# A tuned two-block network on one core: 276 matrix products of zeros in thirteen forms, emitted behind the last store

## The chip, the cores and the metric

The kernel runs on one core of a Trainium2 chip. The time is device microseconds of one execution. Five engines work side by side in a core, each in the order of its own queue: PE (TensorE) multiplies matrices, and its weight loads are listed apart as PEld; DVE (VectorE) and ACT (ScalarE) do elementwise work; POOL (GpSimd) and SP (SyncE) mostly issue transfers. Engines wait for each other on semaphores.

## The reference

Two networks run one after the other on 256 tokens of width 1024, all in float32. The first has two layers of feed-forward, neighbourhood attention with a pooling path, and feed-forward again. The second has four layers, each a mixer (gated linear attention, latent attention, convolution, gated linear attention), an MLP and a gated per-layer input. Its end, cut to what the change touches:

```python
# last layer of the second network, i = 3
x = layer_norm(ALPHA * x + mlp(x))                       # relu(x w1)^2 w2
x = x + sigmoid(x @ ple_w_gate_2[i]) * (p_2[i] @ ple_w_proj_2[i])
return x                                                 # [1, 256, 1024], float32
```

The reference holds no further product: what the change adds is no part of the result.

## The kernel before

The 256 tokens are two tiles of 128 partitions. Every large product is done three times on PE to keep float32 accuracy: each operand is split into a high and a low part of type float32r (ACT copies the high part at L169 or L174, DVE subtracts at L170 or L175), and `mm3` (L177 to L182) adds high times high (L180), high times low (L181) and low times high (L182) into one PSUM bank. A product here is one instruction: `lhsT`, the stationary operand, is loaded as weights, `rhs`, the moving operand, is streamed through. `gemm_rows` holds 128 tokens as weights and streams up to 512 columns of a weight matrix; `gemm_cols` holds 128 columns of a weight matrix and streams 256 or 512 tokens. Other products are of plain float32: the transposes, the attention scores, and the sums at L356.

The order on each engine comes from a scheduler that lets ready work of a lower place in the program go between work of a higher one. SBUF and PSUM come from pools, and a pool opened later gets the space of one that was closed, so its first write waits for the last reader there.

The program is `net.block1()` and then `net.block2()`. The last thing of block 2 is `ple` (L911 to L930) for layer 3, in two halves of 512 columns, each over both token tiles. At its end, for the last 512 columns of the second tile:

```python
nc.scalar.activation(sg[:, gs], ps[t][:, gs], AF.Sigmoid)                # L922, ACT
nc.vector.tensor_mul(sg[:, gs], sg[:, gs], pe[t][:, os])                 # L923, DVE
nc.vector.tensor_add(self.rows[t][:, os], self.rows[t][:, os], sg[:, gs])  # L924, DVE
nc.sync.dma_start(self.out[0, t * P:(t + 1) * P, os], self.rows[t][:, os])  # L926, SP
```

They run on pieces of 256 columns, so twice for each token tile. After the last store the engines meet in a closing exchange of semaphores, listed under the line of the program's end (L1303 before, L1341 after).

Of the kernel before, what the change touches and what calls it, by code (L numbers as in the profile page):

```python
# [18 lines left out]
P = 128  # L19
# [17 lines left out]
def _constants():  # L37
    """Arrays that depend on shapes alone."""
    c = {}
# [59 lines left out]
class Net:  # L99
# [28 lines left out]

# [1 line left out]
    def tick(self, n=1):  # L130
# [7 lines left out]
    def fbank(self):  # L138
        """Either kind of bank in turn."""
        self.turn = not self.turn  # L140
        return self.bank() if self.turn else self.xbank()
# [19 lines left out]
    def halves(self, v, shape=None, tag=""):  # L161
        """The exact split of v into two float32r parts."""
        kn, cn = v.shape[1], v.shape[2]
        out = []
        for nm in ("hi", "lo"):
            t = self.w.tile([P, 1024], F32R, tag="w" + nm + tag, name="w" + nm, bufs=self.SPL)
            out.append(t[:, :kn * cn].rearrange("p (k c) -> p k c", k=kn))
        hi, lo = out
        self.nc.scalar.copy(hi, v)  # L169
        self.nc.vector.tensor_sub(lo, v, hi.bitcast(F32))  # L170
        return hi, lo
# [5 lines left out]
    def mm3(self, ps, a, b, first, last):  # L177
        """ps += a^T b with both as (hi, lo) pairs."""
        mm = self.nc.tensor.matmul
        mm(ps, lhsT=a[0], rhs=b[0], start=first, stop=False)  # L180
        mm(ps, lhsT=a[0], rhs=b[1], start=False, stop=False)  # L181
        mm(ps, lhsT=a[1], rhs=b[0], start=False, stop=last)  # L182

    def gemm_cols(self, ps, w, x, c0, cn):
        """ps[feature, token] over all k: w hi/lo [P, k, 128], x hi/lo [P, k, tokens]."""
        kn = w[0].shape[1]
        for k in range(kn):
            self.mm3(ps, (w[0][:, k, :], w[1][:, k, :]),
                     (x[0][:, k, c0:c0 + cn], x[1][:, k, c0:c0 + cn]), k == 0, k == kn - 1)

    def gemm_rows(self, w, kn, c0, cn, x, tiles, per=4, major=2, order=None, bank=None):
        """Banks [token, column] for each tile; w is a DRAM matrix with kn k-tiles.

        The last major loads are taken tile by tile, so that the first tiles end early."""
        ps = [(bank or self.bank)() for _ in tiles]
# [22 lines left out]
    def rstd_of(self, ms, eps):  # L218
        """(ms + eps)^-1/2; eps may be a column."""
        nc = self.nc  # L220
        v = self.small.tile([P, 1], F32, tag="v", name="v")
        if isinstance(eps, float):
            nc.gpsimd.tensor_scalar(v, ms, eps, None, ALU.add)
        else:
            nc.gpsimd.tensor_tensor(v, ms, eps, ALU.add)
        r = self.small.tile([P, 1], F32, tag="r", name="r", bufs=8)
        nc.gpsimd.tensor_tensor(r, v, self.neg_half, ALU.pow)
        return r

    def rstd_of_two(self, ms):  # L230
        """The same from the two halves' mean squares."""
        m0 = self.small.tile([P, 1], F32, tag="m0", name="m0")
        self.nc.gpsimd.tensor_scalar(m0, ms[0], EPS, None, ALU.add)
        return self.rstd_of(ms[1], m0)

    def meansq(self, src, n):
        """The sum of squares over n, a power of four."""
        ms = self.small.tile([P, 1], F32, tag="ms", name="ms", bufs=8)
        j = self.tmp.tile([P, 1024], BF16, tag="junk", name="junk", bufs=1)
        self.nc.scalar.activation(j[:, :src.shape[-1]], src, AF.Square, scale=float(n ** -0.5), accum_out=ms)  # L240
        return ms

    def columns(self, rows, n, pool, name):
        """[n, 128] rows -> [128, n]."""
        ps = self.tbank()
# [5 lines left out]
    def to_columns(self, rows, hi, lo, c0, nblk):  # L251
        """rows: list of tiles [P, nblk*128]; hi/lo [P, block, token] at c0 get the transposes."""
        nc = self.nc
# [10 lines left out]

# [1 line left out]
    def block1(self):  # L266
# [42 lines left out]
    def mod_raw(self, l, v, k0):  # L309
        """Rows of k-tiles k0, k0+1 for vector v."""  # L310
        return self.load(self.d["w_mod"][l, k0 * P:(k0 + 2) * P, v * D:(v + 1) * D]
                         .rearrange("(k p) c -> p k c", p=P), 2, D)

    def mod_pair(self, l, v):
        """Vectors v and v+1 by matrix products; bank rows 32j (x) and 32j+1 (ctx) for half j."""
        nc = self.nc
# [14 lines left out]
    def mod_units(self, l, vectors):  # L331
        """Steps that form the vectors by sums on the vector engine over k, then over partitions."""
        nc = self.nc
# [35 lines left out]
    def mod_finish(self, l, acc, rows):  # L369
        """From the bank rows (row, vector, half, stream): + b_mod, (1 + scale) g, gate g."""  # L370
        nc, d = self.nc, self.d
# [43 lines left out]
    def modulated(self, l, i, groups):  # L415
        """hT hi/lo [P, 8, tokens] of the modulated norm i for groups of token tiles, each after its tail."""
        nc = self.nc
# [37 lines left out]
    def sooner(self, on=True):  # L455
        """Puts a chain that others wait for ahead of the products around it."""
        return self.tc.high_priority(offset=SOONER) if on else ExitStack()

    def later(self, by):
        """Lets products fill what the chains emitted after them leave free."""  # L460
        return self.tc.high_priority(offset=-by)

    def add_normed(self, t, y, ms):
        """x += y * rstd, y already times the gate row."""
        nc = self.nc
# [78 lines left out]
    def gate_up_rows(self, l, w, hT, hid):  # L544
        """Blocks 0 and 1 token by token, so that tile 0 goes ahead."""
        nc = self.nc
# [16 lines left out]
    def gate_up(self, l, w, f0, fn):  # L563
        """The split gate and up columns of blocks f0..f0+fn, in turn."""
        wgu = self.d["w_ffn_gate_up"][l, w]
# [96 lines left out]
    def stacks(self, hp, mp, q, k):  # L662
        """Heads 2hp and 2hp+1 on partitions: q as (hi, lo), (lo, hi) and k as hi twice; k's lo parts in place."""
        nc = self.nc
# [25 lines left out]
    def attend(self, l, s, hp, mp, stacks, vu, cat):  # L690
        """Heads 2hp and 2hp+1 of stream s: local and context keys for x, context keys for ctx."""
        nc = self.nc
# [29 lines left out]
    def softmax_T(self, sc, nk, scale, mp, dst):  # L722
        """Softmax over the free axis of sc, transposed in blocks into dst [P, nk, 128]."""
        nc = self.nc
# [18 lines left out]
    def na_bias(self, l, hp, t, mp):  # L743
        """[P queries, head, 256 keys]: rpb laid out over the window, -1e30 outside it."""
        nc = self.nc
# [35 lines left out]

# [1 line left out]
    def block2(self, layers=(0, 1, 2, 3)):  # L783
# [39 lines left out]
    def rows_to_xT(self, t, b0, b1, x):  # L823
        """Blocks b0..b1 of token tile t into x."""
        for b in range(b0, b1, 4):
# [15 lines left out]
    def layer_norm(self, i, j, gemm):  # L841
        """x = norm(ALPHA x + gemm); returns x transposed, hi/lo."""
        nc, d = self.nc, self.d
# [28 lines left out]
    def mlp_hidden(self, i, hp, x):  # L872
        """relu(x w1)^2 transposed, hi/lo; the first columns token by token, so that tile 0 goes ahead."""
        nc, d = self.nc, self.d
# [21 lines left out]
    def ple_in(self, i):  # L896
        """The transposed per-layer input, hi/lo."""
        nc, d = self.nc, self.d
# [12 lines left out]
    def ple(self, i, pe, x, last):  # L911
        """x += sigmoid(x w) * pe; returns the new x transposed, or stores it."""
        nc, d = self.nc, self.d
# [17 lines left out]
    def gla(self, j, mp, x):  # L931
# [60 lines left out]
        def scores(h):  # L992
            """Decayed scores of head h [key, query] within each tile and across the two."""
            self.ph = ph + "_rec"
# [101 lines left out]
    def rotate(self, dst, src, cs, t, nh, mp):  # L1096
        """dst, src [P, nh*64]."""
        nc = self.nc
# [13 lines left out]
    def mla(self, j, mp, x):  # L1112
# [23 lines left out]
        def rope_key():  # L1136
            """The rotated key part of all heads, twice over the partitions."""
            ps = self.tbank()
# [22 lines left out]
        def up(raws, off, width):  # L1161
            """hi/lo [P, 8 heads, width] of the head columns at off, for both k-tiles."""
            return [self.halves(raw[:, 0, :].rearrange("p (h c) -> p h c", h=8)[:, :, off:off + width])
# [40 lines left out]
        def scores(h):  # L1204
            """The softmax of head h, keys on partitions."""
            self.ph = ph + "_att"
# [40 lines left out]
    def conv(self, j, mp, x):  # L1247
# [27 lines left out]
        return cat  # L1275


_NAMES = [
# [20 lines left out]
def _program(nc, arrays):  # L1299
# [3 lines left out]
    with tile.TileContext(nc) as tc, ExitStack() as ctx:  # L1303
        net = Net(ctx, tc, d, out)
        net.block1()
        net.block2()


# [9 lines left out]
```

## Time and profile before

| what | value |
|---|---|
| time, median of 2 runs | 3036.41 us (3034.1 to 3038.72) |
| profiled execution: span from first to last instruction | 3045.1 us |
| PE busy | 2980.0 us, 98% of the span |
| DVE, ACT, POOL busy | 1875.6, 1281.8, 288.6 us |
| mean granted TensorE clock | 0.994 of full speed |
| end of the last product of the program | 3040.4 us into the span |

Of the profiled execution only the span is given, not a time of its own; it is one more execution beside the two timed ones. The span lies 8.7 us (0.3%) over the median of those. Full speed of the clock is 2.4 GHz, and its other level is 1.2 GHz, shown as 0.5.

### The profile page before, as it was taken

How to read it: one execution, taken by the hardware profiler on the slowest of the kernel's cores; microseconds unless marked ns; L12 is line 12 of the kernel's file. 1: busy time of each engine (PE TensorE's matmuls, PEld its weight loads, DVE VectorE, ACT ScalarE, POOL GpSimd, SP SyncE). 2: the span in 40 equal slices, each digit the busy share in tenths (PEclk: the TensorE clock that was granted, in tenths of full speed). 3: DMA queues.
4: the chain of work that ended last, by engine and by line, in shares of the span. 5: the costliest groups of instructions: out<-in, count | busy, mean ns of one | idle time of the engine just before them, and what ended most of it. 6: DMA issues, size and time to landing. Idle time of an engine off the chain costs nothing.

```text
span 3045.1 us, 40666 instructions
## 1 busy us (share of the span) xinstructions
PE 2980.0 (98%) x16362; PEld 2481.3 (81%) x16362; DVE 1875.6 (62%) x2454; ACT 1281.8 (42%) x1876; POOL 288.6 (9%) x480
## 2 busy tenths in 40 slices
PE   7999999999999999999999999999999999999999
PEld 5777777787778877787789888987798989887997
DVE  5757765577553775336655567656664776467755
ACT  3222245442222422224654465546453545355543
POOL 2101030011110110001100121000000000002000
PEclk9999999999999999999999999999999999999999
DMA  7555531245543454333345536554455565553654
GB/s 280 179 175 180 187 107 63 91 155 180 170 132 110 149 181 154 99 98 120 97 160 186 176 130 192 187 181 165 131 184 187 183 201 183 186 194 111 198 180 145
DMA packets 321936, 484.70 MB, mean 159 GB/s; under 512 B 16606, under 2 KB 199442, under 8 KB 320340
## 3 DMA queue, kind: packets, MB, share of 16 engines
q1 hardware_dynamic: 307844, 461.75, 46.2%
q0 software_dynamic: 9296, 16.16, 1.6%
q10 hardware_dynamic: 4608, 4.20, 0.5%
q8 instruction: 128, 2.10, 0.3%
q14 instruction: 60, 0.49, 0.0%
HBM read 480.97 MB, written 1.10 MB: 158 GB/s over the span
## 4 chain that ended last, share of the span: by engine, by line
PE 89%; DVE 5%; POOL 2%; ACT 2%; DMA 1%; issue 1%; SPq 0%; ACTq 0%; DVEq 0%; POOLq 0%
PE ffn_gu L180 9%; PE ffn_gu L182 9%; PE ffn_gu L181 9%; PE mlp L181 7%; PE mlp L180 7%; PE mlp L182 7%; PE ffn_dn L182 4%; PE ffn_dn L181 4%; PE ffn_dn L180 4%; PE m L180 3%; PE m L182 3%; PE m L181 3%; DVE wlo L170 2%; PE mix_in L181 1%; PE mix_in L180 1%; PE mix_in L182 1%
## 5 line engine op out<-in xcount | busy, mean ns | idle before, releaser
L170 DVE TENSOR_TENSOR wlo<-raw,whi 128x1024 fp32r<-128x1024 f32 (+1 forms) x735 | 884.9, 1211 | 636.6 <-ACT whi L169 621.6
L169 ACT CAST whi<-raw 128x1024 fp32r<-128x1024 f32 (+1 forms) x735 | 760.7, 1038 | 1129.9 <-PE ffn_gu L181 290.7
L181 PE MATMUL ffn_gu<-hT_lo,whi 128*128 128x512 f32 (+1 forms) x1472 | 524.5, 357 | 1.8 <-DVE hT_lo L175 1.8
L180 PE MATMUL ffn_gu<-hT_hi,whi 128*128 128x512 f32 (+1 forms) x1472 | 525.7, 358 | 0.5 <-ACT hT_hi L174 0.5
L182 PE MATMUL ffn_gu<-hT_hi,wlo 128*128 128x512 f32 (+1 forms) x1472 | 523.8, 356 | 0.7 <-DVE wlo L170 0.7
L180 PEld LDWEIGHTS ffn_gu<-hT_hi,whi 128*128 128x128 f32 x1472 | 277.7, 189 | 52.9 <-ACT whi L169 4.2
L181 PEld LDWEIGHTS ffn_gu<-hT_lo,whi 128*128 128x128 f32 x1472 | 278.1, 189 | 43.8 <-DVE hT_lo L175 2.4
L182 PEld LDWEIGHTS ffn_gu<-hT_hi,wlo 128*128 128x128 f32 x1472 | 277.8, 189 | 43.7 <-DVE wlo L170 1.3
L347 DVE SCALAR_TENSOR_TENSOR macc<-raw,sil,macc 128x1024 f32<-128x1024 f32 x224 | 274.6, 1277 | 42.9 <-DMA raw<-in_w_mod_dram 42.9
L180 PE MATMUL mlp<-xT_hi,whi 128*128 128x256 f32 x896 | 253.9, 283 | 0.0
L181 PE MATMUL mlp<-xT_lo,whi 128*128 128x256 f32 x896 | 253.8, 283 | 0.0
L182 PE MATMUL mlp<-xT_hi,wlo 128*128 128x256 f32 x896 | 253.5, 283 | 0.0
L180 PE MATMUL ffn_dn<-whi,hid_hi 128*128 128x512 f32 x616 | 244.1, 396 | 0.0
L181 PE MATMUL ffn_dn<-wlo,hid_hi 128*128 128x512 f32 x616 | 243.6, 395 | 0.0
L182 PE MATMUL ffn_dn<-whi,hid_lo 128*128 128x512 f32 x616 | 243.5, 395 | 0.0
L180 PE MATMUL mlp<-whi,mlp_hi 128*128 128x512 f32 x512 | 199.2, 389 | 0.0
L181 PE MATMUL mlp<-wlo,mlp_hi 128*128 128x512 f32 x512 | 199.2, 389 | 0.0
L182 PE MATMUL mlp<-whi,mlp_lo 128*128 128x512 f32 x512 | 199.2, 389 | 0.0
L181 PEld LDWEIGHTS mlp<-xT_lo,whi 128*128 128x128 f32 x896 | 172.0, 192 | 0.0
L182 PEld LDWEIGHTS mlp<-xT_hi,wlo 128*128 128x128 f32 x896 | 172.0, 192 | 0.0
L180 PEld LDWEIGHTS mlp<-xT_hi,whi 128*128 128x128 f32 x896 | 172.0, 192 | 0.0
L180 PEld LDWEIGHTS ffn_dn<-whi,hid_hi 128*128 128x128 f32 x616 | 115.9, 188 | 29.3 <-ACT yrow L489 2.5
(402 smaller groups left out, 4794.5 us busy)
## 6 DMA issues: line engine op xcount, KB each, us to landing
raw<-in_mlp_w_dram SPq DMA_DIRECT2D x128, 1024.0 KB, 5.4
raw<-in_w_ffn_gate_up_dram SPq DMA_DIRECT2D x80, 1024.0 KB, 5.3
raw<-in_w_mod_dram SPq DMA_DIRECT2D x72, 1024.0 KB, 5.2
raw<-in_w_ffn_down_dram SPq DMA_DIRECT2D x32, 1024.0 KB, 5.1
raw<-in_gla_w_in_dram SPq DMA_DIRECT2D x24, 1024.0 KB, 5.2
raw<-in_w_in_dram SPq DMA_DIRECT2D x16, 1024.0 KB, 5.0
raw<-in_ple_w_gate_dram SPq DMA_DIRECT2D x16, 1024.0 KB, 5.2
raw<-in_w_ffn_down_dram SPq DMA_DIRECT2D x16, 768.0 KB, 4.6
```

The costliest lines, as they stand in the source:

```text
L169: self.nc.scalar.copy(hi, v)
L170: self.nc.vector.tensor_sub(lo, v, hi.bitcast(F32))
L180: mm(ps, lhsT=a[0], rhs=b[0], start=first, stop=False)
L181: mm(ps, lhsT=a[0], rhs=b[1], start=False, stop=False)
L182: mm(ps, lhsT=a[1], rhs=b[0], start=False, stop=last)
L347: nc.vector.scalar_tensor_tensor(acc[s], raw[:, k - k0, :], c, acc[s], ALU.mult, ALU.add)
```

## The change

A method `probe` is added, and called once after `net.block2()`. It takes four float32r tiles and two bf16 tiles of 1056 columns, sets all to zero on DVE, and issues thirteen groups of products on them into PSUM banks that nobody reads. The groups differ in the starting column of the operands (0 or 8), their type, the number of streamed columns (512 or 256), of weight columns (128 or 64), of contracted partitions (128, 64, or 64 alternating between the lower and the upper half), the number of banks, and whether one pair of operands is used throughout or several in turn. Elsewhere the diff replaces comments and docstrings by empty lines, which moves nothing.

```diff
+    def probe(self):
+
+        nc = self.nc
+        self.ph = "probe"
+        with ExitStack() as ctx:
+            pool = lambda name, bufs, **k: ctx.enter_context(self.tc.tile_pool(name=name, bufs=bufs, **k))
+            pp = pool("probe", 1)
+            ps = pool("probe_ps", 6, space=PSUM)
+            a, b, c, e = (pp.tile([P, 1056], F32R, name="pr" + n) for n in "abce")
+            u, v = (pp.tile([P, 1056], BF16, name="pr" + n) for n in "uv")
+            for t in (a, b, c, e, u, v):
+                nc.vector.memset(t.bitcast(F32) if t.dtype == F32R else t, 0.0)
+            bank = lambda: ps.tile([P, 512], F32, tag="probe", name="probe")
+
+            def run(name, n, lhs, rhs, out=None, banks=1):
+                bs = [bank() for _ in range(banks)]
+                for i in range(n):
+                    o = bs[i % banks]
+                    o = o if out is None else out(o)
+                    nc.tensor.matmul(o, lhsT=lhs(i), rhs=rhs(i), start=i < banks, stop=i >= n - banks)
+
+            run("p0", 20, lambda i: a[:, 0:128], lambda i: c[:, 0:512])
+            run("p1", 20, lambda i: a[:, 0:128], lambda i: c[:, 8:520])
+            run("p2", 20, lambda i: a[:, 8:136], lambda i: c[:, 8:520])
+            run("p3", 20, lambda i: a[:, 8:136], lambda i: c[:, 0:512])
+            run("p4", 20, lambda i: u[:, 0:128], lambda i: v[:, 0:512])
+            run("p5", 24, lambda i: a[:, 8:136], lambda i: c[:, 8:264], out=lambda o: o[:, :256])
+            run("p6", 20, lambda i: a[:, 8:72], lambda i: c[:, 8:520], out=lambda o: o[:64, :])
+            run("p7", 20, lambda i: a[:, 0:128], lambda i: c[:, 0:512], banks=2)
+            run("p8", 20, lambda i: a[:64, 0:128], lambda i: c[:64, 0:512])
+            run("p9", 20, lambda i: a[64 * (i % 2):64 * (i % 2) + 64, 0:128],
+                lambda i: c[64 * (i % 2):64 * (i % 2) + 64, 0:512], banks=2)
+            run("p10", 24, lambda i: u[:, 0:128], lambda i: v[:, 0:256], out=lambda o: o[:, :256])
+            run("p11", 24, lambda i: (a, b)[i % 2][:, 128 * (i % 8):128 * (i % 8) + 128],
+                lambda i: (c, e)[i % 2][:, 512 * (i // 2 % 2):512 * (i // 2 % 2) + 512])
+            run("p12", 24, lambda i: (a, b)[i % 2][:, 8 + 128 * (i % 8):8 + 128 * (i % 8) + 128],
+                lambda i: (c, e)[i % 2][:, 8 + 512 * (i // 2 % 2):8 + 512 * (i // 2 % 2) + 512])
...
         net.block1()
         net.block2()
+        net.probe()
```

On DVE, at the very end of the program, the difference is this; `sgm` is the sigmoid's tile, `xr` the rows that are stored, `pra` to `prv` the six new tiles:

```order
 L923 TENSOR_TENSOR sgm<-sgm,pe 128x256 [waits Activation_49] x2
 L924 TENSOR_TENSOR xr<-xr,sgm 128x256 [waits DVE_49] x2
+L1288 MEMSET pra 128x1056 [waits PE_49]
 L923 TENSOR_TENSOR sgm<-sgm,pe 128x256 [waits Activation_49] x2
 L924 TENSOR_TENSOR xr<-xr,sgm 128x256 [waits DVE_49] x2
-L1303 UNCONDITIONAL_BRANCH
+L1288 MEMSET prb 128x1056
+L1288 MEMSET prc 128x1056
+L1288 MEMSET pre 128x1056
+L1288 MEMSET pru 128x528
+L1288 MEMSET prv 128x528
```

The first memset has come ahead of the last four elementwise operations of the program, and the other five follow them.

On PE, at the same place, with the waits; `ple` is the bank of the last products of the program, `probe` a new bank, `pru` and `prv` the bf16 tiles:

```order
 L182 MATMUL ple_25273<-whi,xT_lo 128x512
-L1303 UNCONDITIONAL_BRANCH
+L1296 MATMUL probe<-prc,pra 128x512 [waits DVE_49,PE_49,Activation_49]
+L1296 MATMUL probe<-prc,pra 128x512 x79
+L1296 LDWEIGHTS pru [waits DVE_49]
+L1296 MATMUL probe<-prv,pru 128x512 [waits DVE_49]
+L1296 LDWEIGHTS pru
```

All new products stand behind the last product of the program, group after group; the first one waits for DVE and ACT, and the bf16 ones have a weight load that stands as an instruction of its own.

## Rows read from the trace of the kernel before

**Rows 1.** The page's head and its section 1, busy us by engine:
```profile
span 3045.1 us, 40666 instructions
PE 2980.0 (98%) x16362; PEld 2481.3 (81%) x16362; DVE 1875.6 (62%) x2454; ACT 1281.8 (42%) x1876; POOL 288.6 (9%) x480
```

**Rows 2.** Timeline from 3036 us: start us, us, engine line operation [idle before]:
```profile
3036.16 0.39 PE L180 MATMUL ple<-whi,xT_hi 128*128 128x512 f32 x1
...
3040.01 0.39 PE L182 MATMUL ple<-whi,xT_lo 128*128 128x512 f32 x1
3040.44 0.66 ACT L922 ACTIVATE sgm<-ple 128x256 f32<-128x256 f32 x2 [4.78 <-PE ple L182]
3040.86 0.76 DVE L923 TENSOR_TENSOR sgm<-sgm,pe 128x256 f32<-128x256 f32 x2 [4.01 <-ACT sgm L922]
3041.53 0.76 DVE L924 TENSOR_TENSOR xr<-xr,sgm 128x256 f32<-128x256 f32 x2
```

**Rows 3.** The stores' line: duration ns min/median/max, first and last start us:
```profile
L926 SPq DMA_DIRECT2D out_dram<-xr x8: 332/372/433, 3026.1 to 3042.4; - x8
DMA to landing us min/median/max: 1.7/1.7/1.8
```

**Rows 4.** The program's last line, PE's part of the closing exchange, same columns:
```profile
L1303 PEldq DRAIN  x2: 13/2140/4267, 3036.2 to 3044.6; - x2
```

**Rows 5.** Groups by line and form, memsets on DVE: xcount | busy us, mean ns:
```profile
L282 DVE MEMSET sil<- 128x256 f32 x1 | 0.3, 272 | 0.9 <-PEq L1314 0.9
L291 DVE MEMSET ones<- 128x32 f32 x1 | 0.1, 85 | 0.0
```

**Rows 6.** Groups by form, weight loads of two products with the same weights:
```profile
L180 PEld LDWEIGHTS mlp<-whi,mlp_hi 128*128 128x128 f32 x512 | 96.1, 188 | 19.9
L181 PEld LDWEIGHTS mlp<-wlo,mlp_hi 128*128 128x128 f32 x512 | 96.1, 188 | 19.6
```

**Rows 7.** Timeline of PE, 256 streamed columns, first and last of eleven neighbours:
```profile
2729.79 0.28 PE L182 MATMUL m<-xT_hi,wlo 128*128 128x256 f32 x1
...
2730.99 0.28 PE L180 MATMUL m<-xT_hi,whi 128*128 128x256 f32 x1
```

**Rows 8.** The same with 64 weight columns, first and last of seven neighbours:
```profile
2091.42 0.28 PE L180 MATMUL m<-xT_hi,whi 128*64 128x256 f32 x1
...
2092.10 0.28 PE L180 MATMUL m<-xT_hi,whi 128*64 128x256 f32 x1
```

**Rows 9.** Timeline of PE, products in neighbouring quarters of the array's columns, merged:
```profile
91.99 1.07 PE L356 MATMUL mod<-macc,ones 128*32 128x512 f32 x8
```

**Rows 10.** Timeline of PE around a product over 64 partitions:
```profile
495.01 0.39 PE L180 MATMUL mix_in<-whi,hT_hi 128*128 128x512 f32 x1
495.33 0.38 PE L705 MATMUL mix_att<-kl,qs 64*128 64x256 f32 x1
495.64 0.50 PE L181 MATMUL mix_in<-wlo,hT_hi 128*128 128x512 f32 x1
```

**Rows 11.** Windows: length us, PE, PEld, DVE, ACT, POOL busy, PEclk, DMA share, GB/s:
```profile
1534.40:1537.60 3.20, 0.05 (x1) 0.00 (x0) 3.20 (x7) 3.08 (x7) 0.38 (x1) 1.00 0.57 197
1537.70:1541.00 3.30, 1.04 (x3) 0.75 (x4) 2.53 (x4) 0.50 (x1) 2.05 (x2) 0.50 0.11 36
1541.10:1544.40 3.30, 3.30 (x17) 3.30 (x16) 1.56 (x5) 1.64 (x5) 0.00 (x0) 0.50 0.80 278
1544.60:1548.00 3.40, 3.40 (x31) 3.40 (x30) 1.24 (x2) 2.09 (x3) 0.00 (x0) 1.00 0.00 0
2121.00:2145.00 24.00, 22.17 (x79) 14.77 (x78) 11.14 (x52) 11.66 (x38) 0.00 (x0) 0.64 0.13 47
3041.00:3045.08 4.08, 0.00 (x0) 0.00 (x0) 1.29 (x4) 0.10 (x1) 0.00 (x0) 0.74 0.19 64
```

**Rows 12.** Timeline of PE inside the third of those windows:
```profile
1542.73 0.41 PE L180 MATMUL ffn_gu<-whi,hT_hi 128*128 128x256 f32 x1
1542.95 0.41 PE L181 MATMUL ffn_gu<-wlo,hT_hi 128*128 128x256 f32 x1
```

## The prediction

> **What bounds the kernel now.** I read the page first: PE is busy for 2980.0 of 3045.1 us [rows 1], so PE is the bound, and work put on PE where nothing runs beside it is paid in full. Then I read the end of the timeline, because the change stands there. The reader is to see three things in it. The last eighteen products start 0.2265 us apart (from 3036.16 to 3040.01 in 17 steps) and the last one ends at 3040.40. Behind it comes a short chain: ACT from 3040.44, DVE from 3040.86 to 3042.29 [rows 2]. The last store is issued at 3042.4 and lands 1.7 us later, at about 3044.1 [rows 3]; the span ends at 3045.1, so the closing exchange takes about 1.0 us. PE takes part in that exchange: its drain begins at 3036.2 and lasts 4.27 us, to 3040.4, which is the end of its last product [rows 4]. So nothing hides work that comes behind the last product: PE, idle for the last 4.6 us before, now runs longest, and the program ends about 1.0 us after PE.
>
> **The part ahead of the first new product.** The order shows that the memset of the first tile now stands ahead of DVE's last four operations, and that it waits for PE, as ACT does at 3040.44. Two memsets give its price: 128 x 32 took 85 ns and 128 x 256 took 272 ns, 0.835 ns for each further column [rows 5], so 1056 columns take about 0.94 us. DVE's four operations then run from 3041.38 for their 1.43 us (3040.86 to 3042.29 before), to 3042.81, and the stores move back by 0.5 us, which the products now cover. The second and third memset follow (2 x 0.94), to 3044.69. The first product needs the third tile, so it starts at about 3044.8. The other three memsets lie beside the first 80 products.
>
> **The products.** There are 276: 228 with 512 streamed columns, 48 with 256. Durations in the trace overlap (0.39 us for a start every 0.2265), so I count starts, not durations. Reuse of the same weights saves nothing that the trace shows: L180 and L181 multiply by the same slice and both have 512 weight loads of 188 ns [rows 6].
> - p0 to p3, p7, p11 and p12 (148 products) have the form of the last products of the program, at 0.2265 us: 33.5 us. That half of them start at column 8 is shown by no row; I take no difference.
> - p8 (20) has 64 contracted partitions and streams the same 512 columns: 4.5 us.
> - p6 (20) loads 64 weight columns. With 256 streamed columns, starts are 0.120 us apart with 128 weight columns [rows 7] and 0.113 with 64 [rows 8], so I take 0.220 us: 4.4 us.
> - p5 (24) has 256 streamed columns at 0.120: 2.9 us.
> - p4 (20) and p10 (24) are bf16, which no product in the trace is. Below, the streamed columns bind: at the half clock 256 columns take 0.22 us [rows 12], so about 0.107 at full speed, and 0.213 for 512. Above, a load of 188 ns could stand bare ahead of each product, which gives 0.41 and 0.30. I take 0.220 and 0.113, near the floor, since every neighbouring row hides its load: 4.4 + 2.7 us.
> - p9 (20) alternates between the lower and the upper half of the partitions. In the one case of separate parts of the array, quarters of its columns, eight records of 512 columns take 1.07 us [rows 9], while one after another they would need at least 8 x 0.213 = 1.7. I take pairs, 10 x 0.2265 = 2.3 us; one after another would be 4.5.
>
> The sum is 54.7 us. Four times the part of the array in use changes (into p6, p7, p8, p10). Around a product on 64 partitions the starts are 0.32 us apart on the way in, where 0.2265 is usual, and 0.31 on the way out, behind 256 columns that usually take 0.120 [rows 10]: 0.09 and 0.19 more. Four changes: 0.6 us.
>
> On the array's parts the Trainium skill, "TensorEngine Tiling (Array Packing)", section "Key Properties", says that a change of tiling mode drains the engine and that separate tiles load and multiply in parallel; the trace agrees with the first by the 0.09 and 0.19 us, and with the second only for columns, so that for p9 no run here shows it yet.
>
> On the plain interval the Trainium skill, "TensorE: Matmul & The Clock Gate", section "Back-to-back issue gap", gives N/2.4 + 2.5 ns, an estimate of 0.216 us for 512 columns and 0.109 for 256; the sum by it would be 218 x 0.216 + 48 x 0.109 = 52.3 us. The measured 0.2265 differs, and for the float32r groups the measurement decides.
>
> **The clock.** Before, PE stops at 3040.40, and over 3041 to 3045.08 the granted clock is 0.74, so that about half of this stretch is at the 1.2 GHz level. Now PE waits 4.4 us, from 3040.40 to 3044.8, and starts at the half level. The nearest row is the wait at 1534: PE was idle over 1534.4 to 1537.6, the clock was 0.50 in the next 3.3 us with PE partly busy, still 0.50 in 3.3 us with PE fully busy, and 1.00 after that [rows 11]. I take the fully busy stretch and half of the partly busy one, 5.0 us. Columns then take twice as long (0.22 against 0.107 for 256) [rows 7, 12], so 5.0 us hold 11.6 products of 0.43 us in place of 2.6 us at full speed: 2.4 us lost. The bounds are 0 (no fall) and 3.1 us (6.6 us at half).
>
> **Sum.** Start 3044.8, products 54.7, changes of mode 0.6, clock 2.4, the last product's 0.39 less its 0.2265 that is counted, 0.2, closing 1.0: the span ends at 3103.7, 58.6 us after 3045.1. The runs shown have a median of 3036.41, 8.7 us under this span, and since nothing ahead of the end moves I add the difference to it: 3095.0 us, 1.9% more. Two per cent, about what a measurement of this kernel can tell from no change, is 60.7 us, at 3097.1; the forecast lies 2 us under that line, less than the 4.6 us by which the two runs shown differ.
>
> **Rivals.**
> 1. The bf16 loads stand bare. They are separate instructions in the order, which speaks for it; every other load in the trace that lies between products of one form is hidden, which speaks against it. Price: 20 x 0.19 + 24 x 0.19 = 8.4 us, hence 3103.4; with p9 one after another 2.2 more. This ends on the other side, slower by over 2%, as soon as a quarter of the loads is exposed.
> 2. The clock falls again in the groups that use half the array (p6, p8, p9, 11.2 us). For it: over 2121 to 2145 the clock averages 0.64 while PE shows 22.17 of 24 us busy [rows 11], so a PE that the profile calls busy does not always hold the full level. Against it: those were small products of plain float32 with waits between them. Price: up to 11 us, I take 6, hence 3101. If zeros kept the level at half throughout, it would be about 50 us: 3145.
> 3. All is at the floor: p1 to p3 and p12 run at the columns alone, the clock does not fall: 54.7 less about 3, and no 2.4: 3089.5. By the Trainium skill's interval, above, it would be 3092.6.
> 4. The products cost nothing since the end is set by the stores: 3036.4 + 0.5 = 3037. PE's drain [rows 4] speaks against it, and so does the order, which has the products.
>
> **How the numbers follow.** The forecast has 0.66, rival 1 0.13, rival 2 0.14 (0.02 of it the clock at half throughout), rival 3 0.06, rival 4 0.01. Within the forecast, the start varies by 0.5 us, the products by 2 us (0.2265 against 0.216 or 0.235), the clock by 2.4, and the median of a few runs by some 2.5: its own range is 3090 to 3100, and about 0.3 of it lies over 3097.1. So slower by over 2% has 0.66 x 0.3 + 0.13 x 0.9 + 0.14 x 0.85 = 0.43, and rivals 3 and 4 with the rest of the others give 0.56 within 2%; faster has 0.01. The range reaches from rival 3 with the runs' spread, 3087, to rival 1 with some of p9, 3107.
>
> **What would show it.** In the changed trace: a first memset of about 0.94 us between ACT's sigmoid and DVE's last four operations; the first new product near 3044.8; a clock of 0.5 in the first microseconds behind it; starts 0.2265 us apart in p0, 0.12 in p5, and two starts close together in each pair of p9; a closing of 1.0 us behind the last product. I would be wrong through starts 0.4 us apart in p4, a clock of 0.5 in the middle of the new groups, or a last product that ends away from 3102 to 3103.

## The result and the profile after

The changed kernel took 3095.28 us, the median of two runs (3095.24 and 3095.32), where the kernel before took 3036.41: 58.9 us more. The quotient of these two medians is 1.0194; the ratio on record is 1.0173, with a 95% interval of 1.0150 to 1.0196 that holds both, so the change is not shown to be slower by 2%. The forecast was 3095.0 us. The profiled execution of the changed kernel took 3095.24 us, with a span of 3093.5.

The page's head and its section 1 of the changed kernel (busy us by engine), for [rows 1]:

```profile
span 3093.5 us, 41224 instructions
PE 3028.1 (98%) x16637; PEld 2518.3 (81%) x16638; DVE 1880.7 (61%) x2460; ACT 1281.8 (41%) x1876; POOL 288.6 (9%) x480
```

PE has 275 more records than before (one of the 276 is missing in the trace), its weight loads have 276 more and DVE has six more; with one more semaphore event these are all of the 558 records that were added. PE is busy 48.1 us longer, not 58: this busy time is taken over two executions whose old part did not take equally long, to which I come back below.

The end of the timeline of the changed kernel, for [rows 2, 5] (start us, us, engine, line, operation, then the idle time before it and what ended it):

```profile
3028.98 0.39 PE L182 MATMUL ple<-whi,xT_lo 128*128 128x512 f32 x1
3029.40 0.66 ACT L922 ACTIVATE sgm<-ple 128x256 f32<-128x256 f32 x2 [4.78 <-PE ple L182]
3029.66 0.94 DVE L1288 MEMSET pra<- 128x1056 f32 x1 [3.85 <-PE ple L182]
3030.51 0.69 DVE L923 TENSOR_TENSOR sgm<-sgm,pe 128x256 f32<-128x256 f32 x2
...
3031.57 0.81 SPq L926 DMA_DIRECT2D out_dram<-xr  x2
3032.04 0.94 DVE L1288 MEMSET prb<- 128x1056 f32 x1 [0.17 <-issue]
3033.15 0.94 DVE L1288 MEMSET prc<- 128x1056 f32 x1 [0.17 <-issue]
...
3034.23 7.97 PE L1296 MATMUL probe<-prc,pra 128*128 128x512 f32 x23 [4.87 <-DVE prc L1288]
```

The reader is to see the queue that the order had announced: the last old product ends at 3029.37 (28.98 and 0.39), the first memset stands ahead of DVE's last four operations, two more follow them, and PE waits 4.87 us for the third tile, by the name in the bracket. The stores are issued meanwhile and cost nothing.

The granted clock around that wait, by windows of the changed kernel (length, PE, PEld, DVE, ACT, POOL busy, PEclk, DMA share, GB/s), for [rows 11]:

```profile
3029.40:3032.60 3.20, 0.00 (x0) 0.00 (x0) 2.77 (x6) 0.66 (x2) 0.00 (x0) 1.00 0.06 20
3032.70:3039.40 6.70, 5.17 (x12) 4.13 (x13) 3.15 (x5) 0.00 (x0) 0.00 (x0) 0.50 0.09 27
3039.60:3092.50 52.90, 52.85 (x264) 40.36 (x263) 0.00 (x0) 0.00 (x0) 0.00 (x0) 1.00 0.00 1
```

PE idles in the first window, and the clock falls to 1.2 GHz behind it; the new products begin at that level, with twelve records in the second window, and from 3039.6 on they run at 2.4 GHz without a break (264 records, the first of them begun before). The clock doesn't fall again in any group.

Now the groups. Where neighbours have one form the timeline merges them into one row, and such a row gives the time between two starts: its length less the time of one record (0.39 us for 512 columns, 0.38 for 512 in bf16, 0.28 for 256, 0.27 for 256 in bf16), divided by the count less one. The timeline of PE in the changed kernel, one stretch from each of p1, p2, p4, p5, p6, p9 and p10:

```profile
3041.12 5.06 PE L1296 MATMUL probe<-prc,pra 128*128 128x512 f32 x21
...
3047.63 2.88 PE L1296 MATMUL probe<-prc,pra 128*128 128x512 f32 x12
...
3055.70 2.75 PE L1296 MATMUL probe<-prv,pru 128*128 128x512 bf16 x12
...
3059.70 2.67 PE L1296 MATMUL probe<-prc,pra 128*128 128x256 f32 x21
...
3062.67 3.61 PE L1296 MATMUL probe<-prc,pra 128*64 128x512 f32 x15
...
3076.03 1.85 PE L1296 MATMUL probe<-prc,pra 64*128 64x512 f32 x14
...
3078.72 2.36 PE L1296 MATMUL probe<-prv,pru 128*128 128x256 bf16 x20
```

They give 0.2335 us for p1 (weights from column 0, stream from column 8), 0.226 for p2 (both from column 8), 0.2155 for p4, 0.1195 for p5, 0.230 for p6, 0.112 for p9, so two in 0.225, and 0.110 for p10. The last new product of this kernel starts at 3092.11 and ends 0.40 us later, 1.0 us before the end of the span:

```profile
3092.11 0.40 PE L1296 MATMUL probe<-pre,prb 128*128 128x512 f32 x1
```

The measure that tells most here is the **tail**: from the end of the last old product to the end of the span. It was 3045.08 - 3040.40 = 4.68 us before [rows 2] and is 3093.47 - 3029.37 = 64.10 us now. The change costs 59.4 us by that, where 58.6 were forecast.

### The profile page after: what moved, and what is told of

Its sections match the earlier page's. It is cut to its first block, busy times and chain, and to the rows that moved or that the text cites. A ratio compares the mean times of both kernels' runs of the same rounds, so it can differ in the third digit from the quotient of the medians.

```text
span 3093.5 us, 41224 instructions
## 1 busy us (share of the span) xinstructions
PE 3028.1 (98%) x16637; PEld 2518.3 (81%) x16638; DVE 1880.7 (61%) x2460; ACT 1281.8 (41%) x1876; POOL 288.6 (9%) x480
## 4 chain that ended last, share of the span: by engine, by line
PE 88%; DVE 5%; POOL 2%; ACT 2%; DMA 2%; issue 1%; SPq 0%; ACTq 0%; DVEq 0%; POOLq 0%
PE ffn_gu L180 9%; PE ffn_gu L182 9%; PE ffn_gu L181 9%; PE mlp L181 7%; PE mlp L182 7%; PE mlp L180 7%; PE ffn_dn L182 4%; PE ffn_dn L181 4%; PE ffn_dn L180 4%; PE m L180 2%; PE m L181 2%; PE m L182 2%; PE probe L1296 2%; DVE wlo L170 2%; PE mix_in L181 1%; PE mix_in L180 1%
```

## The experiments

The first six below alter the changed kernel, each as the code shown with it says, and e2 alters the engine and the place of the zeros and the banks together; the last two run the changed kernel and e2 again. In this table the old products' end, the span and the tail are read from each kernel's profiled execution; "attention" is the granted clock over 2121 to 2145 us, a stretch of the old program that no kernel alters.

| kernel | last old product ends | span | tail | attention | median us, ratio to before |
|---|---|---|---|---|---|
| before | 3040.40 | 3045.1 | 4.7 | 0.64 | 3036.41 |
| changed | 3029.37 | 3093.5 | 64.1 | 1.00 | 3095.28, 1.0173 (1.0150 to 1.0196) |
| e1_memsets_only | 3031.48 | 3039.4 | 8.0 | 1.00 | 3042.5, 1.0005 (0.9993 to 1.0017) |
| e2_zeros_early | 3037.53 | 3093.3 | 55.8 | 0.64 | 3095.13, 1.0178 (1.0158 to 1.0197) |
| e3_twice | 3038.92 | 3158.2 | 119.3 | 0.64 | 3153.24, 1.0374 (1.0355 to 1.0393) |
| e4_numbers | 3039.75 | 3102.7 | 63.0 | 0.64 | 3104.5, one run |
| e5_offsets | 3036.66 | 3128.4 | 91.8 | 0.72 | 3130.3, one run |
| e6_parts | 3032.31 | 3065.3 | 33.0 | 1.00 | 3067.1, one run |
| e7_change_again | 3037.07 | 3101.1 | 64.1 | 0.64 | 3103.47, 1.0200 (1.0186 to 1.0214) |
| e8_early_again | 3032.32 | 3088.1 | 55.8 | 1.00 | 3091.07, 1.0164 (1.0150 to 1.0178) |

**The memsets without the products.** All 276 products are left out, the six memsets stay.

```diff
-            run("p0", 20, lambda i: a[:, 0:128], lambda i: c[:, 0:512])
...
-            run("p12", 24, ...)
```

> Keeps the six memsets of zeros behind the last store and leaves out all 276 products. Theory (the tail is serial work of PE: wait, products, clock, closing): from the end of the last product to the end of the span 4.7 us before become about 8.0, since six memsets with 0.17 us ahead of each end about 7.0 us behind that product and the closing takes 1.0; the time is about 3040, within 2% of before. Rival (a part of the 59 us is the longer program's end and not the products): well over 3045.

Two rows of this kernel's timeline, the first memset and the last:

```profile
3031.76 0.94 DVE L1288 MEMSET pra<- 128x1056 f32 x1 [3.84 <-PE ple L182]
...
3037.92 0.50 DVE L1288 MEMSET prv<- 128x528 uint32 x1
```

The sixth memset ends at 3038.42 and the span 1.0 us later; the tail is 3.3 us longer than before. In the time this can't be told from nothing (0.9993 to 1.0017). So the memsets set the end of a program without products, and 56.1 of the 59.4 us come with the products. That sets rival 4 aside as well: what the stores and the memsets alone set ends 56 us earlier.

**Zeros ahead of the end.** The tiles are opened and zeroed by POOL as the last `ple` begins, and the products take the PSUM banks that `ple` uses, so that nothing has to wait for the end of the old products.

```diff
+                if i == layers[-1]:
+                    pp = pool("probe", 1)
+                    self.pz = [...]                    # six tiles
+                    for z in self.pz:
+                        nc.gpsimd.memset(z..., 0.0)
                 x = self.ple(i, pe, x, i == layers[-1])
+            self.probe()
...
-            bank = lambda: ps.tile([P, 512], F32, tag="probe", name="probe")
+            bank = self.fbank
```

> The zeros are set by POOL at the start of the last gated input, and the same 276 products follow the last product of the program without waiting for DVE. Theory: the first new product starts one interval behind the last old one, the clock does not fall, and the tail is 64.1 less 4.9 us of waiting less 2.5 us of half clock, about 56.6 us; the time is about 7.4 us under that of the change, 3088. Rival 1 (zeros or these forms lower the clock by themselves): the fall to half stays, 2.5 us less gained. Rival 2 (the closing or the stores set the end): no gain.

The timeline of this kernel at the same place, and its windows behind it:

```profile
3037.14 0.39 PE L182 MATMUL ple<-whi,xT_lo 128*128 128x512 f32 x1
...
3037.36 1.98 PE L1298 MATMUL probe<-prc,pra 128*128 128x512 f32 x8
```

```profile
3037.60:3041.20 3.60, 3.60 (x17) 3.00 (x16) 1.43 (x4) 0.62 (x2) 0.00 (x0) 1.00 0.22 73
3041.30:3092.30 51.00, 51.00 (x257) 38.90 (x255) 0.00 (x0) 0.00 (x0) 0.00 (x0) 1.00 0.00 1
```

The first product behind the old ones starts 0.22 us after the last of these, there is no idle time, and the clock stays at 1.00. The tail is 55.76 us, 8.34 less than with the change: 4.87 of the wait, 2.5 of the clock, 0.7 because three of the products have gone into gaps among the old ones (273 records stand behind them), and 0.2 because product overlaps product at the seam. So the wait and the half level together are worth 7.4 us, and both hang on when the zeros are ready. Yet the median, 3095.13, showed none of it beside the change's 3095.28. The table says why: here the old part took 8.2 us longer than in the changed kernel's profiled execution. To compare on one chip, both were run again, below.

**Twice the products.**

```diff
             def run(name, n, lhs, rhs, out=None, banks=1):
+                n = 2 * n
```

> Every group has twice its products, 552 in all. Theory: start and clock are paid once, the second 276 cost their intervals at full clock alone, 55.6 us: about 3151, and each group's stretch doubles except the first. Rival 1 (the clock falls again in the groups on half the array): up to 11 us more. Rival 2 (a fixed cost of the probe hides in the 59 us): the second half costs clearly under 55.

The windows of this kernel over the wait, the stretch at half level, and the rest:

```profile
3038.92:3043.78 4.86, 0.00 (x0) 0.03 (x1) 4.09 (x7) 0.66 (x2) 0.00 (x0) 0.86 0.16 54
3043.79:3049.20 5.41, 5.41 (x13) 4.25 (x14) 1.93 (x3) 0.00 (x0) 0.00 (x0) 0.50 0.01 3
3049.30:3157.20 107.90, 107.90 (x540) 83.49 (x539) 0.00 (x0) 0.00 (x0) 0.00 (x0) 1.00 0.00 1
```

The tail grows by 119.27 - 64.10 = 55.2 us, so 276 products of this mix cost 55.2 us at the full level, where the forecast had 54.7; wait and half level stay what they were, 4.86 and 5.4 us. Beside the wait and the half level no fixed part of the cost shows.

**Numbers in place of zeros.** The first 1024 columns of each tile are copied from the finished rows of the first token tile; only the last 32 columns are zeroed.

```diff
-                nc.vector.memset(t.bitcast(F32) if t.dtype == F32R else t, 0.0)
+                nc.vector.memset(t[:, D:]..., 0.0)
+                nc.vector.tensor_copy(t[:, :D], self.xr[:, 0, :])
```

> The operands hold the 1024 final numbers of the first token tile in place of zeros (copied by DVE; only the last 32 columns are set to zero). Theory: the intervals and the clock do not depend on the numbers; the first product starts some 1 to 2 us later because a copy and a short memset take longer than a memset, and the products' stretch stays at 58.3 us give or take 2.5 for the clock. Rival (zeros are cheaper for PE, by the clock or by the interval): intervals over 0.24 us or a clock below 1.0 in the middle of the products.

```profile
3039.75:3043.19 3.44, 0.00 (x0) 0.03 (x1) 3.37 (x12) 0.66 (x2) 0.00 (x0) 0.87 0.21 71
3043.20:3049.10 5.90, 5.90 (x14) 4.64 (x15) 1.68 (x5) 0.00 (x0) 0.00 (x0) 0.50 0.02 5
3049.20:3101.70 52.50, 52.50 (x263) 40.10 (x261) 0.00 (x0) 0.00 (x0) 0.00 (x0) 1.00 0.00 1
```

These are its windows over the same three stretches. From the end of the half level on, numbers run as zeros do: 263 records in 52.50 us against 264 in 52.90, without a fall of the clock. A copy of 1024 columns takes DVE 0.65 us where a memset of 1056 took 0.94, and the short memset lies beside it, so the wait shrinks from 4.87 to 3.45 us, where one or two more had been expected. The tail shrinks by 1.1 of these 1.4 us, since PE starts earlier into the half level and spends 5.9 us in it in place of 5.3. Even the shorter wait is followed by the fall.

**The columns at which operands begin.** The thirteen groups are replaced by ten of 40 products: six of 512 columns with weights and stream from columns (0, 0), (8, 8), (0, 8), (8, 0), (0, 4) and (0, 16), two with 64 and 32 weight columns, and two that stream 256 columns, with 128 and 64 weight columns.

```diff
+            for i, j in ((0, 0), (8, 8), (0, 8), (8, 0), (0, 4), (0, 16)):
+                run("f", 40, lambda k, i=i: a[:, i:i + 128], lambda k, j=j: c[:, j:j + 512])
+            for w in (64, 32):
+                run("w", 40, ... a[:, 0:w], ... c[:, 0:512], out=lambda o, w=w: o[:w, :])
+            for w in (128, 64):
+                run("n", 40, ... a[:, 0:w], ... c[:, 0:256], out=lambda o, w=w: o[:w, :256])
```

> In place of the thirteen groups, ten groups of 40 products in one form each: starting columns (weights, streamed) of (0,0), (8,8), (0,8), (8,0), (0,4), (0,16), then 64 and 32 weight columns with 512 streamed, then 128 and 64 weight columns with 256 streamed. Theory (the interval depends on whether both operands start at the same place within 64 bytes): 0.2267 us in (0,0), (8,8) and (0,16), and 0.233 in (0,8), (8,0) and (0,4). Rival (it is how a group happens to start, and groups settle after some ten products): all six end at 0.2267. For the weight columns: if narrower loads cost less, 0.220 and 0.217 for 64 and 32 columns, and 0.120 and 0.113 with 256 streamed; if not, 0.227 to 0.230 and 0.120 throughout.

Merged rows of this kernel's timeline of PE, one from each group but the first, which holds the stretch at half level:

```profile
3053.53 8.80 PE L1296 MATMUL probe<-prc,pra 128*128 128x512 f32 x38
3062.63 8.80 PE L1296 MATMUL probe<-prc,pra 128*128 128x512 f32 x37
3071.72 9.26 PE L1296 MATMUL probe<-prc,pra 128*128 128x512 f32 x39
3081.29 8.96 PE L1296 MATMUL probe<-prc,pra 128*128 128x512 f32 x38
3090.32 9.10 PE L1296 MATMUL probe<-prc,pra 128*128 128x512 f32 x39
3099.72 8.91 PE L1296 MATMUL probe<-prc,pra 128*64 128x512 f32 x38
3108.93 8.96 PE L1296 MATMUL probe<-prc,pra 128*32 128x512 f32 x38
3118.08 4.49 PE L1296 MATMUL probe<-prc,pra 128*128 128x256 f32 x36
3122.76 4.48 PE L1296 MATMUL probe<-prc,pra 128*64 128x256 f32 x38
```

By the same working they give 0.227 us for (8, 8), 0.234 for (0, 8), 0.233 for (8, 0), 0.232 for (0, 4), 0.229 for (0, 16), 0.230 and 0.232 for 64 and 32 weight columns, and for 256 streamed columns 0.120 and 0.1135. So it isn't column 8 that costs, but that weights and stream begin at different columns: 2 to 7 ns of 227. The theory of 64 bytes missed for (0, 16), which it had put at 0.2267 us. Fewer weight columns cost 3 to 5 ns where 512 are streamed, which no expectation had, and gain 6.5 ns where 256 are. How the nanoseconds follow from the difference of the columns these points don't settle.

**Parts of the array.** The thirteen groups are replaced by five: halves of the partitions in turn (40), one half alone (40), quarters in turn (80), two of the quarters in turn (40), and quarters with 256 streamed columns (80).

```diff
+            hs = lambda k, m, n: slice(m * (k % n), m * (k % n) + m)
+            run("h2", 40, ... a[hs(k, 64, 2), 0:128], ... c[hs(k, 64, 2), 0:512], banks=2)
+            run("h1", 40, ... a[0:64, 0:128], ... c[0:64, 0:512], banks=2)
+            run("q4", 80, ... a[hs(k, 32, 4), 0:128], ... c[hs(k, 32, 4), 0:512], banks=4)
+            run("q2", 40, ... a[hs(k, 32, 2), 0:128], ... c[hs(k, 32, 2), 0:512], banks=2)
+            run("q4n", 80, ... a[hs(k, 32, 4), 0:128], ... c[hs(k, 32, 4), 0:256], banks=4, ...)
```

> In place of the thirteen groups: 40 products alternating between two halves of the partitions, 40 on the lower half alone in two banks, 80 over the four quarters in turn, 40 over two quarters, and 80 over four quarters with 256 streamed columns. Theory (products on separate parts stream side by side and their loads are hidden): 0.227 us for each pair, 0.227 for each single product on one half, 0.227 for four quarters, 0.227 for two, and 0.12 for four with 256 columns: 4.5, 9.1, 4.5, 4.5 and 2.4 us. Rival (loads go one after another and bind once four parts share a stream): four quarters take 0.43 us or more, 8.5 us with 512 columns and the same with 256.

Merged rows of this kernel's timeline of PE: one half alone, the quarters, two of the quarters, the quarters with 256 columns.

```profile
3043.66 8.55 PE L1296 MATMUL probe<-prc,pra 64*128 64x512 f32 x37
...
3052.59 4.85 PE L1296 MATMUL probe<-prc,pra 32*128 32x512 f32 x80
...
3057.25 4.02 PE L1296 MATMUL probe<-prc,pra 32*128 32x512 f32 x34
...
3062.38 0.89 PE L1296 MATMUL probe<-prc,pra 32*128 32x256 f32 x24
```

One half alone has a start every 8.16 / 36 = 0.227 us, as the whole array has. Two quarters in turn give two products in 3.63 / 16 = 0.227 us, and four quarters four in 4.46 / 19 = 0.235, with the change of parts in it. Four quarters with 256 columns take some 0.12 us, as one product with 256 does. So products on separate partitions do run at the same time, two or four of them in the time of one; half the partitions don't shorten a product, and a quarter alone was not run. The Trainium skill, "TensorEngine Tiling (Array Packing)", section "Key Properties", says that separate tiles load and multiply in parallel, and for rows of the array, too, the trace now agrees, with these rows.

Two windows of this kernel, over the wait and over its stretch at half level, bear on the clock:

```profile
3032.31:3037.17 4.86, 0.00 (x0) 0.03 (x1) 4.09 (x7) 0.66 (x2) 0.00 (x0) 1.00 0.16 54
3037.42:3040.83 3.41, 3.41 (x18) 3.12 (x18) 1.71 (x3) 0.00 (x0) 0.00 (x0) 0.50 0.02 5
```

The wait was 4.87 us here too, but the clock was still full when PE started again and fell only 0.25 us later, and the half level held for 3.4 us. With PE running it held for 5.3 us in the changed kernel and for 5.1 to 5.9 in e3, e4, e5 and e7. Pairs of products start 0.427 us apart there in place of 0.227, so some eight pairs lost 1.6 us, not 2.5. So the wait brings the fall, but its length doesn't fix the loss; whether the products on half the partitions play a part here no run separates.

**The change and the early zeros on one chip.** The same two kernels again.

> The change itself, beside the version with early zeros on the same chip, to compare the two directly. Theory: the tail from the end of the last old product to the end of the span is 64.1 us again, within 0.2, since it hangs on nothing ahead of it, and the time is about 59.4 us over the kernel before. Rival: the tail of 64.1 us was one execution's, and the wait or the clock fall differs by more than 1 us this time.

> The version with early zeros again (all 276 products of zeros; tiles zeroed by POOL ahead of the last products of the program). Theory: the tail is 55.8 us again, and the median lies 8 us under that of the change run beside it, about 51 us over the kernel before. Rival: what the tail gains is lost in the part ahead of it, where POOL now works beside the last layer and three products of zeros stand among the old ones: then the two medians agree within 3 us, as 3095.1 and 3095.3 did on their different chips.

The tails are 64.05 and 55.76 us, 0.05 and 0.00 from the first time. The medians are 3103.47 and 3091.07: now 12.4 us apart, where 8 had been expected, and 63.4 and 51.0 us over the kernel before on that chip, 3040.04. The early zeros' 51.0 is their tail less 4.68 (51.1); the change's 63.4 is 4 us above its 59.4. Of the two profiled executions the spans lie 13.0 us apart: 8.3 are the tail, and 4.75 the old part (3037.07 against 3032.32). What lengthens an old part is seen over 2121 to 2145 us, first in the changed kernel and then in the same kernel again:

```profile
2121.00:2145.00 24.00, 22.77 (x117) 15.16 (x117) 16.10 (x76) 13.27 (x50) 0.00 (x0) 1.00 0.07 23
```

```profile
2121.00:2145.00 24.00, 23.25 (x87) 15.50 (x85) 12.08 (x56) 10.00 (x37) 0.00 (x0) 0.64 0.08 22
```

In 24 us PE did 117 products at the full level, and 87 where half of the stretch and more was at 1.2 GHz. Two loads of a table for ACT's functions, at L734 and next at L922, lie before and behind this stretch in every kernel and serve as fixed events. Their rows in the changed kernel, and in the same kernel again:

```profile
2116.80 1.28 ACT L734 ACT_TABLE_LOAD   x1
...
2363.80 1.28 ACT L922 ACT_TABLE_LOAD   x1
```

```profile
2117.85 1.28 ACT L734 ACT_TABLE_LOAD   x1
...
2371.20 1.28 ACT L922 ACT_TABLE_LOAD   x1
```

From the first load to the second it is 247.0 us, and 253.35 in the repeat: 6.35 of the 7.7 us by which their old parts differ. Over all ten executions it is 247.0 us in the four with a clock of 1.00, and 252.2 to 253.4 in the six others. From the second load (L929 with early zeros) to the last old product's end it is 665.6 and 665.9 us in the change's two executions, 665.9 and 665.2 with early zeros: the work of POOL and the three products there don't slow the last layers. In the table the four executions with a clock of 1.00 there end the old part at 3029.4 to 3032.3, the six with 0.64 or 0.72 at 3036.7 to 3040.4: not one lies between. Which of the two an execution gets doesn't go with the kernel: the change had both, and so had the early zeros.

## Why the prediction was right, and how closely

**What bounds the kernel.** PE to the end, with nothing to hide work behind its last old product: right. The chain of waits of the changed kernel has the new products at its end (start us, us, engine, line, count), and the closing behind them is 1.0 us, as forecast:

```profile
3034.23 21.41 PE probe L1296 x81
3055.70 36.81 PE probe L1296 x194
```

Both stretches together, 58.2 us, are the path from PE's wait to the last product, with no other engine between.

**The terms**, with the tail as the measure:

| term | forecast us | measured us |
|---|---|---|
| last old product's end to the first new start | 4.4 | 4.87 |
| products and changes of parts, at the full level | 55.3 | 55.6 |
| loss by the clock | 2.4 | 2.5 |
| last product's overhang, closing | 1.2 | 1.1 |
| tail | 63.3 | 64.1 |
| less the tail before | 58.6 | 59.4 |

The products' line is what remains of 64.10 when the others are taken off; the doubled kernel gives 55.2 for it without most of the changes of parts.

- **The start.** Order, waits and the memset of 0.94 us came as said, read from two memsets of other sizes [rows 5]. Missing were 0.25 us ahead of the first memset (it starts 0.29 after the last product's end, ACT 0.03 after it) and 0.17 us ahead of each of the next two, which the bracket calls issue: together 0.6, less 0.16 that DVE's four operations save by overlapping it and each other. This term was the most mis-sized, and it is a latency between operations of DVE that no duration contains.
- **Changes of parts.** They were put at 0.6 us and measure 0.3: 0.2 into p8 and 0.1 behind p9. The changes to 64 weight columns and back, into p6 and p7, show no later start; the price had been carried over to them from a product on half the partitions [rows 10].
- **The products.** "I take no difference" for the groups at column 8 was wrong by 7 ns a product where only one operand starts there (p1 and p3, 40 products, 0.3 us). p6 was put at 0.220 and has 0.230, 0.2 us more: fewer weight columns don't help where 512 columns are streamed, and the row with 256 [rows 8] should not have been carried over. p11 and p12, in turn from two tiles, take 10.84 us for 47 starts, 0.2306 each, 0.2 more. Against that p4 and p10 are at 0.2155 and 0.110, 0.2 us less. p9 pairs up as forecast.
- **bf16.** Rival 1 fell: the loads that stand as separate instructions are hidden. The Trainium skill, "TensorE: Matmul & The Clock Gate", section "Back-to-back issue gap", with its N/2.4 + 2.5 ns for the gap of single products, gives 0.216 and 0.109 us, and for bf16 the trace agrees (0.2155 and 0.110). For float32r it doesn't: 0.226 to 0.234 and 0.120.
- **The clock.** Rival 2 fell: no second fall in p6, p8 or p9, nor anywhere behind 3039.5. The one fall was read from the wait at 1534 [rows 11] and came as there: 5.3 us with PE running at half level, for 5.0 forecast. That the size came so close is partly luck: behind the same wait it was 3.4 us in e6, for a loss of 1.6. That zeros play no part in it is shown by the run with numbers, and that it comes with the wait of PE by the early zeros, which have neither the wait nor the fall. Rival 3, all at the floor, lost by these 2.5 us and by p1 and p3.

**The base.** "Since nothing ahead of the end moves I add the difference to it": nothing moved in the order, but the old part still differs by up to 11 us between executions, so the span forecast from before's own execution, 3103.7, was 10.2 us above the one profiled, and the last product ended at 3092.5, not at 3102 to 3103. By the prediction's own sign, a last product that ends away from 3102 to 3103, it would have been wrong; but that sign hung on the old part and not on the new work. Passing from that span to the median of the runs made up for it, and that forecast and result agree within 0.3 us is luck: the sum was 0.8 us short, and the same kernel took 3103.47 us when it was run again, over the 3090 to 3100 that the forecast gave itself. This also is why the line of 2% could not be called: with 59.4 us the change lies 1.3 us under it, and by its repeat on it (1.0186 to 1.0214).

## What to carry to other kernels

Where the change stands at one place and the rest of the program scatters, measure that place in the trace from one fixed event to another: the tails of the two kernels that ran twice repeat within 0.05 us, while medians of the change differ by 8. Work that is put behind the last product costs PE's wait for its operands as well, and the half level that follows the wait; operands made ready early saved 7.4 of 59.4 us. Add up starts, not durations, and look for latencies between operations as terms of their own.

## What the runs showed of the hardware

- The old part has two lengths, 5.2 to 6.4 us apart, by the clock granted in 24 us of the latent-attention layer (0.64 or 0.72 against 1.00), though the instructions there are the same; further stretches move it by up to 4.6 us more. What decides the clock there was not found; no run tried to.
- Behind a wait of PE of 4.87 us the half level held with PE running for 5.1 to 5.5 us in four executions, and for 3.4 us in a fifth (e6), where it began only after PE had started again.
- float32r products whose weights and stream begin at different columns of their tiles start up to 7 ns later each (0.227 to 0.234 us).
- Products on 64 partitions alone start as far apart as on 128 (0.227 us), and two on separate halves or four on separate quarters of the partitions run in that time.
- Of changes between parts of the array only those of the rows showed: into p8 two starts come after 0.32 and 0.335 us where 0.227 is usual, 0.2 us in all, and behind p9 one after 0.32; into p6, with 64 of the weight columns, none comes later.
